# The heaviest expert's tokens 97 to 128: out of the overflow branch of their pair and into plain code

## The chip, the cores and the metric

The kernel runs on one core of a Trainium2 chip. The metric is the device time of one execution in microseconds (us), lower is better. The engines are named as in the profile: PE (TensorE matmul), PEld (its weight loads), DVE (VectorE), ACT (ScalarE), POOL (GpSimd), SP (SyncE, which here only issues DMAs).

## The reference, cut to what matters

Two layers; each is a mixer (convolutions in layer 0, gated MLP and attention in layer 1) and then a mixture of experts over 512 tokens of 1024 channels. Only the mixture is touched.

```
g_prob = softmax(xt @ rg_w + rg_b);  g_top, g_idx = top_k(g_prob, 1)     # 4 groups
e_top, e_idx = top_k(softmax(logits of the 8 experts of that group), 2)  # 2 experts a token
weights = g_top * e_top / sum(e_top)
...
hb = silu(xb @ w_gate[e]) * (xb @ w_up[e])     # 1024 -> 512
yb = hb @ w_down[e]                            # 512 -> 1024
y  = sum over the token's two experts of weight * yb
x  = LN(alpha * x + y)
```

All is float32. There are 32 experts; one has 3 matrices of 2 MB. How many tokens an expert gets is known only when the kernel runs.

## The kernel before, in words

A layer's 32 experts are taken in 16 pairs (`for g in range(NP)` in `experts`, L1056). A pair has a table of 128 slots. In twelve pairs each of the two experts has 64 slots. In the four pairs with column `COLS[g]` of at least `HEAVY` = 12, a heavily loaded expert (e = 0) has 96 slots and a lightly loaded one (e = 1) has 32. The experts are ordered by load at run time, so the heaviest of all (outside the first two pairs, which are fixed) is e = 0 of column 12, which is worked at g = 7.

In a pair PE runs, in this order: the gate projection (`proj2("g")`, 64 matmul instructions of 32 columns in a heavy pair), the up projection (`proj2("u")`), the adding of the previous pair's result into `acc` (`combine`: PE spreads rows by a one-hot matrix S, DVE adds), the transposes of the hidden rows in the middle of that (`hidden_T`), then the overflow branch `tc.If(v > 0)` (L1120), then the down projection (`down`) in two halves with the transposes of the next pair's tokens (`gather_T`) between them.

Tokens beyond the slots have a second table T2. `counts` (L621) writes into `nxi`, for each pair, 0 (nothing exceeds), 1 or 2 (one expert exceeds by up to 32) or 3 (more). If the value is over 0 the branch runs `overflow(v)`: it transposes the rows gathered into `xg2` (`gather2`, itself in a branch on POOL, one pair ahead), then either the full width (`wide`: `proj8`, `down8`) or one expert on 32 rows with the matrices cut into four strips that work side by side (`single(e)`: `proj1`, L840; `down1`, L881; `added1`, L872 and L875). The same code is emitted for g = 2 to 15 in both layers; a hint for PE's instruction fetch stands ahead of the up projection.

Weights come through a ring of nine 2 MB slots (`Stream`): matrix n of the sequence (six for a pair) takes the place of matrix n - 9. SP issues the loads in order, and a load waits until the last instruction that could read the old matrix has passed. The branch may read any of the pair's matrices, so a pair's two gate matrices and two up matrices are given back when PE has passed the branch, and the down matrices after the second half of `down`. What is given back at the branch of pair g are the places of the second up matrix and both down matrices of pair g + 1 and the first gate matrix of g + 2.

Of the kernel before, what the change touches and what calls it, by code (L numbers as in the profile page):

```python
# [7 lines left out]
F32 = mybir.dt.float32  # L8
# [35 lines left out]
def trunk(ctx: ExitStack, tc: tile.TileContext, a, out, layers=2, moe=True):  # L44
# [21 lines left out]
    def small(shape, name, dt=F32, **kw):  # L66
        return wk.tile([128] + list(shape), dt, name=name, **kw)
# [374 lines left out]
    class Router:  # L442
# [178 lines left out]
        def counts(self):  # L621
            c = self.rk[:, NT]
            big = wk.tile([128, NE, NE], F32, name="big", tag="xb")
            TT(big, self.at, bc(c[:, None, :], [NE, NE]), op=OP.mult)
            cs = small([NP, 2], "cs", tag="rcb")
            DVE.tensor_reduce(cs.rearrange("p g two -> p (g two)"), big, axis=AX.X, op=OP.add)
            over = small([2, NP, 2], "over", tag="scr")
            for i in range(2):
                TT(over[:, i], cs, lim[:, i], op=OP.is_gt)
            nxs = small([2 * NP + 1], "nxs")  # L630
            n, m = nxs[:, 0:NP], nxs[:, NP:2 * NP]
            mxc = small([NP], "mxc", tag="mxc")
            DVE.tensor_reduce(mxc, over[:, 1], axis=AX.X, op=OP.max)
            DVE.scalar_tensor_tensor(n, over[:, 0, :, 1], 2.0, over[:, 0, :, 0], op0=OP.mult, op1=OP.add)
            DVE.scalar_tensor_tensor(n, mxc, float(WIDE), n, op0=OP.mult, op1=OP.max)
            mxe = small([NP], "mxe", tag="mxc")
            DVE.tensor_reduce(mxe, c.rearrange("p (g two) -> p g two", two=2), axis=AX.X, op=OP.max)
            nx = small([NP, NTHR], "nx", tag="scr")
            TT(nx, bc(mxe[:, :, None], [NP, NTHR]), bc(thr[:, None, :], [NP, NTHR]), op=OP.is_gt)
            DVE.tensor_reduce(m, nx, axis=AX.X, op=OP.add)  # L640
            for g in FIRST:
                DVE.scalar_tensor_tensor(m[:, g:g + 1], mxe[:, g:g + 1], float(CAP), m[:, g:g + 1], op0=OP.is_gt, op1=OP.add)
            DVE.tensor_reduce(nxs[:, 2 * NP:], m, axis=AX.X, op=OP.max)
            nxi = small([2 * NP + 1], "nxi", I32)
            DVE.tensor_copy(nxi, nxs)
            return nxi
# [59 lines left out]
    def gather_T(src, gb, xt=None):  # L706
        xt = slots_T() if xt is None else xt
        transposed(src, lambda h, p: put_T(xt, gb, h, p))
        return xt
# [123 lines left out]
    def blocks4(p, f):  # L833
        for c in range(4):
            f(p[SUB * c:SUB * c + SUB], c)

    def proj1(tag, x, w, e):
        p = ptile(tag, (128, 128))
        for k in range(KD):
            blocks4(p, lambda o, c: PE.matmul(o, x[:, k, SUB * e:SUB * e + SUB], w[:, k, 128 * c:128 * c + 128],  # L840
                                              start=(k == 0), stop=(k == KD - 1)))
        return p
# [45 lines left out]
    def down8(hT, ww, wt, tk, own):  # L888
        S = onehot_S(tk)
        y = wk.tile([128, 2, 512], F32R, name="y2", tag="xb")  # L890
        ys = [(y[:, 0], y[:, 1]), tuple(wk.tile([128, 512], F32R, name="y3" + t, tag=t) for t in ("r", "q1"))]
        for h in range(2):
            scaled_parts(*ys[h], proj8("gu"[h], hT, ww, own, 4, slice(512 * h, 512 * h + 512)), wt)
        for h in range(2):
            for t in range(NT):
                added(t, h, S, ys[h])
# [76 lines left out]
    def when(nxi, i, above, engines=None):  # L973
        v = count(nxi, i, **({} if engines is None else {"engines": engines}))
        return v, tc.If(v > above)

    def experts(rt, ws, T1, pt, x1d, xt, xg, xg2, update, last, last2, lead, finish):
# [46 lines left out]
        def col(t, g):  # L1024
            return t[:, COLS[g]:COLS[g] + 1]

        def gather2(g):
            with when(nxi, COLS[g], 0, [ET.Pool])[1]:
                gather(xg2, x1d, col(T2.idx, g))

# [25 lines left out]
        for g in range(NP):  # L1056
            W = lambda j: ws.u[6 * g + j]
            own, own2 = EVEN if COLS[g] < HEAVY else ODD
            if g == NP - 1:
                crowded()  # L1060
                last()
            skip = f"skip{ws.l}_{g}"
            sg = gated(proj2("g", xt, W(0), W(1), own))
            if g == 0:
                onehot2()
            if g < 2:
                ws.load(6 * g + 2 + 9)
            tw = small([2], "tw")

            def either(v, wide, single):  # L1070
                with tc.If(v > WIDE - 1) as c:
                    wide()
                with c.Else():
                    with tc.If(v > 1) as c1:
                        single(1)
                    with c1.Else():
                        single(0)

            def overflow(v):
                h2 = wk.tile([128, 512], F32, name="h2", tag="r")  # L1080
                xo = gather_T(xg2, rt.gb, wk.tile([128, KD, 128], F32, name="xo", tag="xb"))
                hT2 = wk.tile([128, 4, 128], F32, name="hT2", tag="q0")

                def wide():
                    ACT.activation(h2, proj8("g", xo, (W(0), W(1)), own2), AF.Silu)
                    DVE.tensor_mul(h2, h2, proj8("u", xo, (W(2), W(3)), own2))
                    hidden2_T(h2, hT2, 4)

                def single(e):
                    b = (0, 1) if own2 == EVEN[1] else (2, 1)  # L1090
                    s = slice(0, 128)
                    ACT.activation(h2[:, s], proj1("g", xo, W(e), b[e]), AF.Silu)
                    DVE.tensor_mul(h2[:, s], h2[:, s], proj1("u", xo, W(2 + e), b[e]))
                    hidden2_T(h2, hT2, 1)
                    r = slice(SUB * b[e], SUB * b[e] + SUB)
                    for i, src in enumerate((T2.tk, T2.wt)):
                        blocks4(tw, lambda o, c: DVE.tensor_copy(o[:, i:i + 1], col(src, g)[r]))
                either(v, wide, single)
                either(v, lambda: down8(hT2, (W(4), W(5)), col(T2.wt, g), col(T2.tk, g), own2),
                       lambda e: down1(hT2, W(4 + e), tw[:, 1:2], tw[:, 0:1]))  # L1100
            if g:
                S = onehot_S(col(T1.tk, g - 1))
                if g == NP - 1:
                    combine(S, *prev, (0, 1))
            if g > 1:
                v = count(nxi, COLS[g])
                tc.mark_branch_hint_location(skip, v > 0, engines=[ET.PE])
            pu = proj2("u", xt, W(2), W(3), own)
            h = hidden(sg, pu)
            if g == 0:  # L1110
                first_weights()
            else:
                combine(S, *prev, range(2 if g == NP - 1 else 0, CM if g < NP - 1 else NT))
            hT = hidden_T(h)
            if g == 0:
                ws.ids = rt.order()
            if 0 < g < NP - 1:
                combine(S, *prev, range(CM, NT))
            if g > 1:
                with tc.If(v > 0, label=skip, preferred_fallthrough_block=True):  # L1120
                    overflow(v)
            ws.load(6 * g + 4 + 9)
            if g == NP - 1:
                last2()
            if 0 < g < NP - 1:
                gather2(g + 1)
            if g == NP - 2:
                most = count(nxi, 2 * NP)
                tc.mark_branch_hint_location(f"most{ws.l}", most > 0, engines=[ET.PE])
            if g == NP - 1:  # L1130
                S = onehot_S(col(T1.tk, g))
            if g < NP - 1:
                wt = wt0 if g == 0 else col(T1.wt, g)
                y = down(hT, W(4), W(5), wt, halves=(0,), own=own)
                xt = gather_T(xg, rt.gb)
                if g == 0:
                    nxi, rest = picks()
                if g + 2 < NP:
                    gather(xg, x1d, col(T1.idx, g + 2))
                prev = down(hT, W(4), W(5), wt, y, (1,), own)  # L1140
                if g == 0:
                    rest()
            else:
                end, y = Last(lead), None
                for h in range(2):
                    y = down(hT, W(4), W(5), col(T1.wt, g), y, (h,), own)
                    end.half(h, S, *y)
            ws.load(6 * g + 6 + 9)
# [525 lines left out]
```

## Time and profile before

| | us |
|---|---|
| three runs | 1456.77, 1446.28, 1455.97 (median 1455.97) |
| profiled execution: its own time | 1450.72 |
| profiled execution: its span | 1448.9 |

The profiled execution lies between the lowest and the highest of the three runs. Times below are us from the start of its span. Layer 0's experts fill about 203 to 690 us, layer 1's about 947 to 1420. A row of the timeline gives start, length, engine, line, operation, tiles written and read, the count of merged instructions, and in brackets how long the engine was idle before it and what ended that.

### The profile page before, as it was taken

How to read it: one execution, taken by the hardware profiler on the slowest of the kernel's cores; microseconds unless marked ns; L12 is line 12 of the kernel's file. 1: busy time of each engine (PE TensorE's matmuls, PEld its weight loads, DVE VectorE, ACT ScalarE, POOL GpSimd, SP SyncE). 2: the span in 40 equal slices, each digit the busy share in tenths (PEclk: the TensorE clock that was granted, in tenths of full speed). 3: DMA queues.
4: the chain of work that ended last, by engine and by line, in shares of the span. 5: the costliest groups of instructions: out<-in, count | busy, mean ns of one | idle time of the engine just before them, and what ended most of it. 6: DMA issues, size and time to landing. Idle time of an engine off the chain costs nothing. (4 is left out here: it accounts for less than half of the span.)

```text
span 1448.9 us, 19205 instructions
## 1 busy us (share of the span) xinstructions
PE 1326.9 (92%) x7119; PEld 698.7 (48%) x7121; DVE 675.9 (47%) x1387; ACT 368.3 (25%) x694; POOL 294.0 (20%) x261
## 2 busy tenths in 40 slices
PE   9989999998978999988899999999998999988984
PEld 6767764343333433333576767744433343333331
DVE  7998588232222332232718555784322232322336
ACT  5545631111101111111524455521111111111101
POOL 5785610000000000000463229300000000000002
PEclk9999999999998999999999999999999999999997
DMA  7505479999997899999700018789999999999971
GB/s 293 232 5 241 166 262 425 420 424 422 420 400 301 355 426 423 422 420 378 283 1 1 23 66 325 268 320 423 421 423 424 423 423 422 425 421 422 420 304 59
DMA packets 56693, 461.19 MB, mean 318 GB/s; under 512 B 8661, under 2 KB 9301, under 8 KB 33089
## 3 DMA queue, kind: packets, MB, share of 16 engines
q1 hardware_dynamic: 51184, 449.96, 75.4%
q0 software_dynamic: 4464, 7.79, 1.5%
q8 instruction: 101, 1.65, 0.5%
q10 hardware_dynamic: 864, 1.13, 0.2%
q14 instruction: 80, 0.65, 0.1%
HBM read 461.04 MB, written 6.29 MB: 323 GB/s over the span
## 5 line engine op out<-in xcount | busy, mean ns | idle before, releaser
L745 PE MATMUL pu<-w,xt 128*64 128x512 f32 (+1 forms) x1280 | 247.8, 606 | 31.8 <-DMA w<-in_w_up_dram 31.8
L745 PE MATMUL py<-w,hT 128*64 128x512 f32 (+1 forms) x1280 | 242.3, 611 | 18.4 <-issue 7.3
L745 PE MATMUL pg<-w,xt 128*64 128x512 f32 (+1 forms) x1280 | 235.1, 600 | 10.9 <-ACTq L1033 10.9
L760 DVE TENSOR_TENSOR h<-sg,pu 128x512 f32<-128x512 f32 x32 | 22.0, 688 | 379.9 <-issue 342.7
L690 POOL DMA_INDIRECT xg<-x1d,idx x29 | 28.7, 990 | 794.3 <-PE m L439 711.6
L745 PEld LDWEIGHTS pu<-w,xt 128*64 128x64 f32 (+1 forms) x1280 | 75.4, 129 | 194.1 <-issue 149.0
L798 DVE TENSOR_TENSOR acc<-acc,m 128x512 f32<-128x512 f32 x240 | 148.6, 680 | 17.9 <-PE m L790 15.7
L745 PEld LDWEIGHTS pg<-w,xt 128*64 128x64 f32 (+1 forms) x1280 | 77.5, 127 | 163.4 <-issue 144.6
L745 PEld LDWEIGHTS py<-w,hT 128*64 128x64 f32 (+1 forms) x1280 | 71.7, 128 | 150.7 <-issue 146.8
L779 DVE SCALAR_TENSOR_TENSOR y<-py,wt,y 128x512 fp32r<-128x512 f32 x64 | 48.0, 750 | 194.6 <-ACT y L778 194.6
L778 ACT ACTIVATE y<-py,wt 128x512 fp32r<-128x512 f32 x64 | 44.0, 687 | 295.1 <-PE py L745 295.1
L789 PE MATMUL m<-y,S 128*128 128x512 f32 x248 | 106.2, 428 | 0.0
L109 POOL TENSOR_TENSOR wl<-win,wh 128x512 fp32r<-128x512 f32 x64 | 84.5, 1335 | 67.7 <-ACT wh L108 67.5
L790 PE MATMUL m<-y,S 128*128 128x512 f32 x248 | 97.8, 394 | 0.0
L768 ACT ACTIVATE hT<-m 128x512 f32<-128x512 f32 x32 | 19.1, 598 | 304.9 <-PE m L766 282.9
L109 POOL TENSOR_TENSOR wl<-wo,wh 128x512 fp32r<-128x512 f32 x64 | 82.3, 1314 | 34.8 <-ACT wh L108 34.4
L755 ACT ACTIVATE sg<-pg 128x512 f32<-128x512 f32 x32 | 19.1, 597 | 219.0 <-PE pg L745 219.0
L789 PEld LDWEIGHTS m<-y,S 128*128 128x128 f32 x248 | 46.6, 188 | 39.7 <-issue 26.9
L128 PE MATMUL m<-xh,wl 128*128 128x512 f32 x144 | 58.7, 408 | 3.1 <-POOL wl L109 3.1
L127 PE MATMUL m<-xh,wh 128*128 128x512 f32 x144 | 58.3, 405 | 0.8 <-ACT wh L108 0.8
L129 PE MATMUL m<-xl,wh 128*128 128x512 f32 x144 | 57.9, 402 | 0.0
L108 ACT ACTIVATE wh<-win 128x512 fp32r<-128x512 f32 x64 | 38.9, 625 | 49.0 <-PE pg L129 13.4
(445 smaller groups left out, 1858.8 us busy)
## 6 DMA issues: line engine op xcount, KB each, us to landing
w<-in_w_gate_dram SPq DMA_DIRECT2D x64, 2048.0 KB, 25.0
w<-in_w_up_dram SPq DMA_DIRECT2D x50, 2048.0 KB, 18.3
w<-in_w_down_dram SPq DMA_DIRECT2D x50, 2048.0 KB, 21.2
w<-in_w_up_dram SPq DMA_DIRECT2D x40, 512.0 KB, 24.7
w<-in_w_down_dram SPq DMA_DIRECT2D x40, 512.0 KB, 22.3
win<-in_w_in_dram SPq DMA_DIRECT2D x18, 512.0 KB, 7.6
wo<-in_w_out_dram SPq DMA_DIRECT2D x4, 2048.0 KB, 12.2
w<-in_w_up_dram SPq DMA_DIRECT2D x8, 1024.0 KB, 16.2
```

Of the source, the lines that this page charges most:

```text
L108: ACT.activation(h, src, AF.Copy)
L109: POOL.tensor_tensor(l, src, h, op=OP.subtract)
L127: PE.matmul(p, wh[:, j], xh[:, k], start=(k == 0), stop=False)
L128: PE.matmul(p, wl[:, j], xh[:, k], start=False, stop=False)
L129: PE.matmul(p, wh[:, j], xl[:, k], start=False, stop=(k == KD - 1))
L690: POOL.indirect_dma_start(out=dst, out_offset=None, in_=x1d, in_offset=bass.IndirectOffsetOnAxis(ap=idx_col, axis=0), bounds_check=T - 1, ...
L745: PE.matmul(p[w * c:w * c + w], x[:, w * c:w * c + w], ww[own[w * c // SUB]], **kw)
L778: ACT.activation(yh[:, s], p, AF.Copy, scale=wt)
L779: DVE.scalar_tensor_tensor(yl[:, s], p, wt, yh[:, s], op0=OP.mult, op1=OP.subtract)
L789: PE.matmul(p, S[:, t * 128:(t + 1) * 128], yh[:, s], start=start, stop=False)
L790: PE.matmul(p, S[:, t * 128:(t + 1) * 128], yl[:, s], start=False, stop=True)
L798: DVE.tensor_add(acc[:, t, s], acc[:, t, s], p)
```

## The change

For column 12 (`top`), e = 0 of T2 is always computed in plain code, spread over iteration g = 7: the gather is no longer in a branch; the copies of token numbers and weights (`single_in`), the transposes of the gathered rows and `proj1` for the gate come between the gate and the up projection; `proj1` for the up matrix, the product and one transpose come between `hidden_T` and the rest of `combine`; `down1` comes after `combine`, ahead of the branch. The branch stays, with the full width only, for the case that e = 1 exceeds its 32 slots; it then leaves out the block that the plain code has done. `counts` gets one more small instruction, which sets the value of column 12 to 3 if e = 1 exceeds and else to 0.

```
+            TS(n[:, HEAVY:HEAVY + 1], over[:, 0, HEAVY:HEAVY + 1, 1], float(WIDE), None, op0=OP.mult)
...
         def gather2(g):
+            if COLS[g] == HEAVY:
+                gather(xg2, x1d, col(T2.idx, g))
+                return
...
+            top = COLS[g] == HEAVY
+            def single_in(e):
+                b = ((0, 1) if own2 == EVEN[1] else (2, 1))[e]
+                for i, src in enumerate((T2.tk, T2.wt)):
+                    blocks4(tw, lambda o, c: DVE.tensor_copy(o[:, i:i + 1], col(src, g)[SUB * b:SUB * b + SUB]))
+                return b
...
             def either(v, wide, single):
+                if top:
+                    wide()
+                    return
...
+            if top:
+                b = single_in(0)
+                xo = gather_T(xg2, rt.gb, wk.tile([128, KD, 128], F32, name="xo", tag="xb"))
+                h2 = wk.tile([128, 128], F32, name="h2", tag="r")
+                ACT.activation(h2, proj1("g", xo, W(0), b), AF.Silu)
             if g > 1:
                 v = count(nxi, COLS[g])
                 tc.mark_branch_hint_location(skip, v > 0, engines=[ET.PE])
...
             hT = hidden_T(h)
+            if top:
+                DVE.tensor_mul(h2, h2, proj1("u", xo, W(2), b))
+                p2 = ptile("g", (128, 128))
+                PE.transpose(p2, h2, ident)
+                hT2 = wk.tile([128, 1, 128], F32, name="hT2", tag="q0")
+                ACT.activation(hT2[:, 0], p2, AF.Copy)
...
             if 0 < g < NP - 1:
                 combine(S, *prev, range(CM, NT))
+            if top:
+                down1(hT2, W(4), tw[:, 1:2], tw[:, 0:1])
             if g > 1:
                 with tc.If(v > 0, label=skip, preferred_fallthrough_block=True):
                     overflow(v)
```

## Rows read from the trace of the kernel before

**Rows 1.** The page: GB/s in 40 equal slices of the span (36.2 us each).

```profile
GB/s 293 232 5 241 166 262 425 420 424 422 420 400 301 355 426 423 422 420 378 283 1 1 23 66 325 268 320 423 421 423 424 423 423 422 425 421 422 420 304 59
```

**Rows 2.** SP's waits in layer 0's experts (us in total, times, longest).

```profile
SPq L964 <- PEq L1120: 141.6, 11, 19.3
```

**Rows 3.** Windows: length, busy time of engines, PEclk, DMA share, GB/s.

```profile
422.00:434.00 12.00, 6.74 (x129) 5.49 (x129) 1.48 (x10) 0.55 (x2) 0.00 (x0) 0.72 0.88 350
...
450.00:461.00 11.00, 11.00 (x78) 3.61 (x72) 3.17 (x7) 2.77 (x6) 0.99 (x1) 0.97 0.40 129
467.00:479.00 12.00, 11.85 (x57) 5.78 (x54) 5.56 (x9) 0.77 (x2) 0.00 (x0) 1.00 0.37 130
...
202.64:653.66 451.02, 417.54 (x2413) 172.16 (x2411) 164.02 (x326) 60.55 (x122) 17.04 (x17) 0.97 0.96 399
946.51:1381.18 434.67, 405.79 (x2215) 164.63 (x2216) 156.11 (x307) 58.85 (x118) 16.00 (x16) 0.99 0.99 414
```

**Rows 4.** Timeline of SP: weight loads; a long merged row ends with the second load.

```profile
398.79 29.94 SPq L964 DMA_DIRECT2D w<-in_w_up_dram  x2
...
433.40 23.70 SPq L964 DMA_DIRECT2D w<-in_w_gate_dram  x2
457.61 17.84 SPq L964 DMA_DIRECT2D w<-in_w_up_dram  x2
...
1145.12 18.45 SPq L964 DMA_DIRECT2D w<-in_w_up_dram  x2
```

**Rows 5.** Timeline of the branch at g = 7 in layer 0.

```profile
418.01 1.05 PE L439 MATMUL m<-ident,xg 128*128 128x128 f32 x8
...
419.46 1.36 DVE L704 TENSOR_SCALAR xo<-m,gb 128x128 f32<-128x128 f32 x4
...
424.67 3.64 PE L840 MATMUL pg<-w,xo 128*32 128x128 f32 x64 [5.60 <-issue]
...
430.72 1.50 PE L840 MATMUL pu<-w,xo 128*32 128x128 f32 x44 [1.15 <-issue]
...
432.34 0.29 DVE L1093 TENSOR_TENSOR h<-h,pu 128x128 f32<-128x128 f32 x1 [11.53 <-PE pu L840]
...
437.10 3.60 PE L881 MATMUL m<-w,hT 128*32 128x256 f32 x32 [4.08 <-issue]
...
444.55 1.82 PE L872 MATMUL m<-y,S 32*128 32x256 f32 x8 [1.37 <-DVE acc L875]
446.29 5.83 PE L745 MATMUL py<-w,hT 128*32 128x512 f32 x32
```

**Rows 6.** Timeline of PE and PEld: pair g = 7, up projection to branch, both layers.

```profile
404.63 1.03 PE L745 MATMUL pu<-w,xt 128*32 128x512 f32 x4
...
406.74 7.06 PE L745 MATMUL pu<-w,xt 128*32 128x512 f32 x60 [1.08 <-DMA w<-in_w_up_dram]
...
413.73 0.50 PE L789 MATMUL m<-y,S 128*128 128x512 f32 x1
...
1151.66 0.16 PEld L745 LDWEIGHTS pu<-w,xt 128*32 128x32 f32 x8 [0.92 <-DMA w<-in_w_up_dram]
...
1158.65 0.50 PE L789 MATMUL m<-y,S 128*128 128x512 f32 x1
...
1163.25 3.64 PE L745 MATMUL py<-w,hT 128*32 128x512 f32 x32
```

**Rows 7.** Windows in the branch, for PEclk (the third figure from the end).

```profile
424.60:428.30 3.70, 3.63 (x70) 3.36 (x73) 0.00 (x0) 0.00 (x0) 0.00 (x0) 0.50 0.79 332
430.70:432.30 1.60, 1.50 (x44) 1.23 (x43) 0.00 (x0) 0.00 (x0) 0.00 (x0) 1.00 0.99 410
```

**Rows 8.** The gather for g = 7 in layer 0, and its time from issue to landing.

```profile
390.23 0.99 POOL L690 DMA_INDIRECT xg<-x1d,idx  x1 [22.43 <-DVE acc L798]
...
xg<-x1d,idx POOLq DMA_INDIRECT x1, 7.3
```

**Rows 9.** Timeline of PE: after a branch that was not taken, g = 4, layer 0.

```profile
328.28 2.78 PE L745 MATMUL py<-w,hT 128*32 128x512 f32 x10 [3.38 <-PEq L1120]
```

More of the change, by code (lines that the diff above doesn't have):

```diff
@@ L1082, in overflow @@
                 hT2 = wk.tile([128, 4, 128], F32, name="hT2", tag="q0")
+                tk2, wt2 = col(T2.tk, g), col(T2.wt, g)
+                if top:
+                    rest2 = small([2], "rest2", tag="mxc")
+                    DVE.memset(rest2, 0.0)
+                    for b in (0, 1, 3):
+                        r = slice(SUB * b, SUB * b + SUB)
+                        DVE.tensor_copy(rest2[r, 0:1], tk2[r])
+                        DVE.tensor_copy(rest2[r, 1:2], wt2[r])
+                    tk2, wt2 = rest2[:, 0:1], rest2[:, 1:2]
                 def wide():
@@ L1089, in single @@
                 def single(e):
-                    b = (0, 1) if own2 == EVEN[1] else (2, 1)
+                    b = single_in(e)
                     s = slice(0, 128)
-                    ACT.activation(h2[:, s], proj1("g", xo, W(e), b[e]), AF.Silu)
-                    DVE.tensor_mul(h2[:, s], h2[:, s], proj1("u", xo, W(2 + e), b[e]))
+                    ACT.activation(h2[:, s], proj1("g", xo, W(e), b), AF.Silu)
+                    DVE.tensor_mul(h2[:, s], h2[:, s], proj1("u", xo, W(2 + e), b))
                     hidden2_T(h2, hT2, 1)
-                    r = slice(SUB * b[e], SUB * b[e] + SUB)
-                    for i, src in enumerate((T2.tk, T2.wt)):
-                        blocks4(tw, lambda o, c: DVE.tensor_copy(o[:, i:i + 1], col(src, g)[r]))
                 either(v, wide, single)
-                either(v, lambda: down8(hT2, (W(4), W(5)), col(T2.wt, g), col(T2.tk, g), own2),
+                either(v, lambda: down8(hT2, (W(4), W(5)), wt2, tk2, own2),
                        lambda e: down1(hT2, W(4 + e), tw[:, 1:2], tw[:, 0:1]))
@@ L1118, in experts @@
                 combine(S, *prev, range(CM, NT))
+            if top:
+                down1(hT2, W(4), tw[:, 1:2], tw[:, 0:1])
             if g > 1:
```

## The prediction, made before the changed kernel was run

> **What bounds the kernel now.** First the row of GB/s: in both expert stages the core moves 420 to 426 GB/s in almost every slice [rows 1]. One matrix of 2.097 MB then takes 4.95 us, a pair of six 29.7 us, and whatever PE does within that costs nothing. The exception is three slices of layer 0 (400, 301, 355), some 400 to 507 us. Second, SP's waits: inside the experts it waits longest for PE's branch [rows 2], so weights are late only when PE is late at that branch. Third, that stretch in windows. At 424 GB/s the three holes lost 12 x 74 / 424 = 2.1 us, 11 x 295 / 424 = 7.7 us and 12 x 294 / 424 = 8.3 us [rows 3], 18.1 us together. As a check: from the first gate matmul to the last group of weight loads layer 0 took 451.02 us and layer 1 434.67 [rows 3], 16.4 us less for the same work. So the loss goes through to the end, and 16.4 to 18.1 us is all that can be won.
>
> Fourth, SP's timeline ties each hole to a release. The second up load of pair 8 went out only at 428.73 (398.79 + 29.94), just as the first gate projection of the branch had ended; the load after the first gate matrix of pair 9 at 457.1; the second up load of pair 9 at 475.45 [rows 4]. The branch was taken only in layer 0, in the arm for e = 0 alone: `single`'s 128-column form of L840 stands there once, and layer 1 goes on to `down` 4.6 us after its up projection, as any skipped pair [rows 5, 6]. So the change replaces a taken branch in layer 0 and adds computation in layer 1, where none ran.
>
> **What it removes.** In layer 0 PE left `combine` at 418 us and reached `down` at 446.29. Of these 28 us, 5.60, 1.15 and 4.08 are idle time put down to "issue" [rows 5], with no data outstanding: PE had no instructions. Plain code should have none of that: 10.8 us.
>
> [...]
>
> **What it adds ahead of the release.** The gate and up matrices of pair 7 still go back only when PE has passed the branch, since the branch can still read them; and all new PE work stands ahead of it. I count PE's delay to that point.
>
> A1, before the up projection: the eight transposes and the ACT and DVE copies took 420.82 - 418.01 = 2.8 us from first to last, and PE has nothing else to do meanwhile; then 64 instructions of `proj1`, which took 1.50 / 44 = 34 ns each at full clock and 3.64 / 64 = 57 ns at half clock [rows 5, 7]. At full clock 2.2 us, sum 5.0 us. Part of it fills a wait: PE idled for the up matrix 1.7 us in layer 0 (406.74 - 404.63 less four instructions of 0.11) and 0.9 us in layer 1 [rows 6]. Net 3.3 and 4.1 us. The lower bound is 1 us less, if `proj1` starts on the first copied slices.
>
> A2, after `hidden_T`: 64 x 34 ns = 2.2 us, the wait for DVE's product (0.29 us and a hand-over [rows 5]) and one transpose: 3.0 us.
>
> A3, `down1`'s 32 matmuls: they took 3.60 us in the branch, like the first `proj1` after an idle time. Their strips have 256 columns, and the 512-column ones of the pair's up projection take (413.73 - 406.74) / 60 = 0.117 us [rows 5, 6], so half of that at full clock, 1.9 us.
>
> A4, from the end of `down1` (440.70) to `down` (446.29): 5.6 us [rows 5]. It holds ACT's and DVE's scaling and eight additions on DVE, whose pace made PE wait 1.37 us for a bank. None of it is branching but the last jump; I take 5.2 us, between 4.6 (full clock, no jump) and 5.6.
>
> Sum 13.4 us in layer 0, 14.2 in layer 1. Without overflow work the second up load of pair 8 would go out 4.60 + 0.32 us after 413.73, at 418.65 [rows 4, 6]; now it goes out at 432.05. That is 3.3 us later than the 428.73 which cost 2.1 us: a hole of 5.4 us. In layer 1 the up matrix landed at 1151.66; the point like 428.73 is 22.0 us later (428.73 - 406.74), 1173.65. The release moves from 1163.57 to 1177.8, 4.1 us past that point: a hole of 6.2 us where there was none.
>
> A second hole shouldn't follow. At the release four loads go out and two more after `down`, 29.7 us of traffic, and PE needs less for a pair: even with a slow start it came from 446.29 to the release of 475.45 in 29.2 us [rows 4, 5]. The margin is thin, and a rival rests on it.
>
> **What is priced at nothing.** The gather on POOL is issued a pair ahead and landed 7.3 us after 390.23 in layer 0, at 397.5, while the transposes now want it at about 404.6 [rows 6, 8]: 7 us of cover; if that goes, PE waits ahead of A1, and the release with it. In layer 1 it is new: 1 us of POOL, which waits 22 us idle, and at most 0.5 MB (1.2 us of traffic at 424 GB/s; most slots there are empty and move nothing, so I take 0). The small DVE instruction in `counts`: at most a few tenths, once a layer, while PE is busy and DMA full. The eight tiny copies on DVE sit behind the gate projection, when DVE is idle. The branch's skip stays as it was.
>
> **Sum.** 18.1 removed, 5.4 and 6.2 added: 6.5 us gained; 4.8 by the check of 16.4. I take 6. Against the profiled execution's own 1450.72 us (span 1448.9, 1.8 around it) that is 1444.7. The four times at hand, 1446.3 to 1456.8, have their middle at 1453.3, which gives 1447; I forecast 1446. A measurement of this kernel can tell about 1% (14.5 us) from no change.
>
> **Rivals.**
>
> (a) The new work overlaps better: `proj1` runs slice by slice behind the copies and the additions drain while `combine` still runs, so that PE is 3 us earlier per layer. The holes fall to 2.4 and 3.2 us, the gain rises to 12.5: about 1438 on the profiled execution. For it: DVE and ACT have room there. Against: the last additions need `down1`'s result, and only their banks set PE's pace.
>
> (b) The new work runs slower than I take it: PEclk is 0.50 as in the branch [rows 7]. A1, A2 and A3 then cost 1.5, 1.5 and 1.7 us more, the holes grow by 4.7 each, and the gain is -2.9: 1453.6. Or PE's skip is not fetched in time, as once in layer 0 (3.38 us [rows 9]); the hint now stands some 250 PE instructions further ahead of it. In one layer the gain is 3.1, in both -0.3. Against half clock: in the trace it came after PE had been idle for 5.6 us, and here it is never idle for 3.
>
> [...]
>
> (c) Slower: the clock falls in A1 to A4 as in (b) and stays down through `down` of pair 7, so that PE misses the thin margin and a second hole opens in each layer. `down`'s first half took 5.83 us there against 3.64 [rows 5, 6]; both halves slow cost 4.4 us, less 0.5 of margin: about 4 us a layer on top of (b), 1461. It decides if the release comes later than about 436 us in layer 0.
>
> (d) The change doesn't do what it says: the branch is taken as well, since e = 1 exceeds 32. The arm taken in the trace was that for e = 0 alone, so the value now is 0. Some 25 us on top, 1470.
>
> **How the numbers follow.** The forecast (a gain of 3 to 10 us) has 0.58, (a) 0.17, (b) 0.18, (c) 0.05, (d) 0.02. From (a), 1438 or a little under, to (b) with the higher of the base times, the range is 1436 to 1457. Faster by over 1% needs a gain of 14.5 us, nearly all there is: the far part of (a), and the spread of the base times, 0.16. Slower by over 1%: (c), (d) and the spread, 0.08. Within 1%: 0.76.
>
> **What would show it.** Right: no idle "issue" of some us at g = 7 in layer 0; holes in GB/s after the branch of g = 7 in both layers, about 5 us each, and none a pair later; SP's second up load of pair 8 about 13 us after the point of a skipped pair; layer 0's experts 13 us shorter and layer 1's 6 us longer. Wrong: no hole in layer 1 (then A1 to A4 are hidden, and the gain nears 17); a hole of 9 us or more (clock or fetch); or a release that no longer waits for the branch.

## The result, and the profile after

| | before | after |
|---|---|---|
| median of 8 runs each, us | 1456.28 | 1442.19 |
| lowest to highest, us | 1446.28 to 1457.60 | 1439.13 to 1445.43 |
| profiled execution: its own time (span), us | 1450.72 (1448.9) | 1442.83 (1440.9) |

The ratio is 0.9929, with a 95% interval of 0.9909 to 0.9948: 10 us (8 to 13) faster. That is a gain, but under the 1% that the prediction set as its bound for faster. The medians lie 14.1 us apart, because five of the eight runs of before stand at 1456 to 1458 us and three at 1446 to 1451; the text goes by the ratio on record and its interval. The two profiled executions differ by 7.9 us.

The page's row of GB/s has lost the dip of layer 0 [rows 1]:

```profile
GB/s 294 234 5 212 175 243 428 419 424 422 419 403 412 422 419 426 422 418 354 206 1 1 23 133 315 257 338 421 420 425 424 421 394 420 427 422 422 423 301 59
```

What is left of it is a shallow place (403, 412), and layer 1 has a new one (394). In windows of 10 us, around g = 7 in each layer, and over each layer's experts from the first gate matmul of the first pair to that of the last:

```profile
204.06:655.10 451.04, 420.16 (x2446) 174.97 (x2445) 167.61 (x337) 64.14 (x131) 16.98 (x17) 0.98 0.99 411
...
420.00:430.00 10.00, 7.36 (x74) 5.14 (x74) 7.54 (x14) 0.75 (x2) 0.00 (x0) 0.96 0.95 401
430.00:440.00 10.00, 9.85 (x67) 3.71 (x69) 4.14 (x9) 2.08 (x5) 0.99 (x1) 0.69 0.87 344
440.00:450.00 10.00, 10.00 (x60) 3.14 (x54) 1.21 (x3) 1.28 (x2) 0.00 (x0) 1.00 1.01 400
...
936.20:1384.82 448.62, 421.48 (x2447) 173.47 (x2446) 167.53 (x337) 64.09 (x131) 17.10 (x17) 0.98 0.99 412
...
1160.00:1170.00 10.00, 8.43 (x56) 3.80 (x60) 5.27 (x10) 1.70 (x5) 0.47 (x1) 0.83 0.84 323
1170.00:1180.00 10.00, 10.00 (x62) 3.15 (x56) 2.19 (x6) 1.11 (x4) 0.52 (x1) 1.00 1.00 413
```

Below, the "hole" of a layer is the sum of (424 - GB/s) x length / 424 over the windows below full rate. Here it is (23 + 80 + 24) x 10 / 424 = 3.0 us in layer 0, where before lost 18.1 [rows 3], and (101 + 11) x 10 / 424 = 2.6 us in layer 1, where before lost nothing. Measured between the same two gate matmuls, layer 0 took 463.7 us before (201.73 to 665.46) and 451.1 now, layer 1 446.6 (946.51 to 1393.08) and 448.6. So layer 0 gave 12.6 us and layer 1 took back 2.1. The first expert matmul also started 2.3 us later (204.06 against 201.73, behind work that the change doesn't touch); 12.6 - 2.1 - 2.3 = 8.2 us, where the two spans differ by 8.0, and the stretches between the layers and behind them agree within 0.3 us.

PE's timeline at g = 7 in layer 0, where [rows 5] showed the branch:

```profile
405.82 1.09 PE L439 MATMUL m<-ident,xg 128*128 128x128 f32 x8
407.07 2.35 PE L841 MATMUL pg<-w,xo 128*32 128x128 f32 x64 [0.16 <-ACT xo L703]
409.23 7.32 PE L746 MATMUL pu<-w,xt 128*32 128x512 f32 x64
...
418.05 1.95 PE L841 MATMUL pu<-w,xo 128*32 128x128 f32 x64
420.49 0.33 PE L1146 MATMUL pg<-ident,h 128*128 128x128 f32 x1 [0.48 <-DVE h L1144]
...
423.55 1.93 PE L882 MATMUL m<-w,hT 128*32 128x256 f32 x32
426.13 0.90 PE L873 MATMUL pg<-y,S 32*128 32x256 f32 x2 [0.65 <-ACTq L1156]
...
429.24 1.81 PE L873 MATMUL m<-y,S 32*128 32x256 f32 x8 [1.37 <-DVE acc L876]
```

No idle time of PE is put down to "issue" here. `down` follows at 431.20, and the release shows on SP's own timeline (the merged row ends with the second up load of pair 8, as in [rows 4]):

```profile
402.15 29.36 SPq L965 DMA_DIRECT2D w<-in_w_up_dram  x2
...
1134.31 28.91 SPq L965 DMA_DIRECT2D w<-in_w_up_dram  x2
```

402.15 + 29.36 = 431.51 in layer 0, 1163.22 in layer 1. And something is there that before didn't have: two issue waits of PE in the last pairs of layer 0, g = 13 and 14. An issue wait, below, is idle time of PE that the profile puts down to "issue" or to PEq, PE's sequencer.

```profile
611.77 2.31 PE L746 MATMUL py<-w,hT 128*32 128x512 f32 x17 [3.23 <-issue]
...
642.37 2.73 PE L746 MATMUL py<-w,hT 128*64 128x512 f32 x10 [2.72 <-issue]
```

### The profile page after: what moved, and what is told of

Read it like the earlier page. It is cut to its first block, busy times and chain, and to the rows that moved or that the text cites. A ratio compares the mean times of both kernels' runs of the same rounds, so it can differ in the third digit from the quotient of the medians.

```text
span 1440.9 us, 19633 instructions
## 1 busy us (share of the span) xinstructions
PE 1333.4 (93%) x7322; PEld 705.9 (49%) x7322; DVE 684.5 (48%) x1412; ACT 370.3 (26%) x701; POOL 294.7 (20%) x262
## 3 DMA queue, kind: packets, MB, share of 16 engines
q0 software_dynamic: 4608, 7.79, 1.5%
## 5 line engine op out<-in xcount | busy, mean ns | idle before, releaser
L746 PE MATMUL pu<-w,xt 128*64 128x512 f32 (+1 forms) x1280 | 244.2, 607 | 19.8 <-DMA w<-in_w_up_dram 19.8
L746 PEld LDWEIGHTS pu<-w,xt 128*64 128x64 f32 (+1 forms) x1280 | 78.3, 129 | 176.3 <-issue 143.2
L799 DVE TENSOR_TENSOR acc<-acc,m 128x512 f32<-128x512 f32 x240 | 148.6, 680 | 19.3 <-PE m L791 17.3
L790 PEld LDWEIGHTS m<-y,S 128*128 128x128 f32 x248 | 46.8, 189 | 39.3 <-issue 26.9
L791 PEld LDWEIGHTS m<-y,S 128*128 128x128 f32 x248 | 46.9, 189 | 7.9 <-DVE y L780 1.0
```

Of the source, the lines that this page charges most:

```text
L746: PE.matmul(p[w * c:w * c + w], x[:, w * c:w * c + w], ww[own[w * c // SUB]], **kw)
L790: PE.matmul(p, S[:, t * 128:(t + 1) * 128], yh[:, s], start=start, stop=False)
L791: PE.matmul(p, S[:, t * 128:(t + 1) * 128], yl[:, s], start=False, stop=True)
L799: DVE.tensor_add(acc[:, t, s], acc[:, t, s], p)
```

## The experiments

Theory 1 is the prediction's: the loss is the hole that PE's lateness at the release of g = 7 makes in the weight traffic; only what stands ahead of the release counts. Its rivals: (2) only the waits in the taken branch counted (5.60, 1.15 and 4.08 us), and the computation is hidden anyway; (3) what counts is PE's whole lag against the loads already issued, wherever in the pair it arises. A last theory (L) came up on the way: some issue waits depend on where the code lies, not on what it does. Ratios are against the kernel before on the same chip, with the 95% interval; 0.1% is 1.45 us.

**No overflow work at all.** The kernel before, with the counts' new line alone; the heaviest expert's tokens 97 to 128 are left out.

```
+            TS(n[:, HEAVY:HEAVY + 1], over[:, 0, HEAVY:HEAVY + 1, 1], float(WIDE), None, op0=OP.mult)
```

> The kernel before, with the count of column 12 set so that its branch is never taken: it leaves out the heaviest expert's tokens 97 to 128 in layer 0, so it bounds what can be won. Theory 1 (the whole loss is the holes in the weight traffic, 18 us before and 5 to 6 in the changed kernel): 16 to 18 us under the kernel before, ratio 0.988, 5 us under the changed kernel, no hole in either layer. Theory 2 (the gain is the fetch stalls of the taken branch, 10.8 us, and the computation itself is hidden): about the changed kernel's time, ratio 0.9925.

Measured: 1438.99 us, ratio 0.9888 (0.9867 to 0.9910). Windows at g = 7 in layer 0:

```profile
420.00:430.00 10.00, 9.91 (x80) 3.55 (x82) 4.22 (x10) 2.77 (x6) 0.99 (x1) 1.00 1.00 424
430.00:440.00 10.00, 7.64 (x32) 2.39 (x30) 0.26 (x1) 0.60 (x1) 0.00 (x0) 0.93 1.00 420
```

No hole. Layer 0 took 446.7 us, layer 1 446.3: 17.0 us less than before in layer 0. That is all there is to be won, and after stands 4.4 and 2.3 us above it. Theory 2 would have put this kernel level with after. Against theory 2 this run alone says little: its interval touches that of after (up to 0.9910, from 0.9909), and below, with the code moved, after comes down to 446.8 us in layer 0 as well. The run with the plain code in one piece decides.

**The change in layer 0 alone.** Layer 1 keeps the branch, which is never taken there. The new lines in `counts` and `gather2` get the same condition.

```
-            top = COLS[g] == HEAVY
+            top = COLS[g] == HEAVY and not ws.l
```

> The change in layer 0 alone; layer 1 keeps the branch, which isn't taken there. Theory 1: the hole of about 2.7 us in layer 1 goes, the rest stays: 2 to 3 us under the changed kernel, ratio 0.991. Theory 2 (new work in layer 1 is hidden): the changed kernel's time, ratio 0.993.

Measured: 1444.03 us, ratio 0.9936 (0.9914 to 0.9957); no better than after. Layer 1's hole was gone (419 and 426 GB/s there), but its stage took 448.1 us against 448.6; it had an issue wait of 3.14 us near the layer's end (at 1343.99) that after didn't have. So this run doesn't price the hole of layer 1, and no theory so far foresaw it. Layer 0 took 454.6 us, 3.5 more than in after, although its hole was the same 2.9 us (352, 392 and 406 GB/s); it too has waits at g = 13 and 14, of 3.25 and 2.37 us. That is where theory L began.

**All of the plain code in one piece ahead of the branch.** The same work at the place where the branch had it, without the jump: nothing overlaps the pair's own projections.

```
             if 0 < g < NP - 1:
                 combine(S, *prev, range(CM, NT))
+            if top:
+                b = single_in(0)
+                ...
+                ACT.activation(h2, proj1("g", xo, W(0), b), AF.Silu)
             if top:
                 DVE.tensor_mul(h2, h2, proj1("u", xo, W(2), b))
```

> All of the new plain code in one piece ahead of the branch, behind combine, not spread over the iteration. Theory 1: PE now stands idle for the copies, no longer fills its wait for the up matrix, and reaches the branch some 3 us later in each layer; the holes grow by as much: 5 to 6 us over the changed kernel, ratio 0.997. Theory 2 (only the fetch stalls mattered): the changed kernel's time, ratio 0.993.

Measured: 1448.63 us, ratio 0.9972 (0.9954 to 0.9991). The interval lies apart from that of after (up to 0.9948), where theory 2 expected the same time. The profiled execution was the fastest of twelve (1443.06 us), so the stages and holes of this kernel are those of its best case. Windows, layer 0:

```profile
420.00:430.00 10.00, 7.74 (x177) 4.96 (x169) 3.88 (x15) 1.41 (x5) 0.00 (x0) 1.00 0.77 324
430.00:440.00 10.00, 8.47 (x57) 3.79 (x60) 5.34 (x10) 1.64 (x5) 0.40 (x1) 0.83 0.64 234
```

The hole is 6.8 us in layer 0 and 7.6 in layer 1. Against before this is the cleanest look at the jump: same work, same place, and the hole went from 18.1 to 6.8, by 11.3 us where the three waits in the branch had been 10.8. PE reached `down` 35.7 us after the pair's first gate matmul, 12.9 us sooner than in before (48.6); what goes beyond the 10.8 is mostly faster matmuls, as those of `down1` (1.93 us here, 3.60 in the branch). The hole also stands elsewhere. In before the taken branch gave its matrices back from inside, one after the other, so before lost only 2.1 us at this release and 16.0 behind it [rows 3, 4]; here the release came when PE had passed the branch, at 433.28, and the whole hole stands there. Against after this kernel shows what the spreading is worth: some 6 us by the ratios, but only 2.2 us by the stages of the profiled executions (451.2 and 450.7 us against 451.1 and 448.6).

**`down1` behind the branch.** 7.7 us of PE's time (423.55 to 431.20 in after) move past the release. The edit also gives `hT2` another buffer.

```
-            if top:
-                down1(hT2, W(4), tw[:, 1:2], tw[:, 0:1])
             if g > 1:
                 with tc.If(v > 0, label=skip, preferred_fallthrough_block=True):
                     overflow(v)
+            if top:
+                down1(hT2, W(4), tw[:, 1:2], tw[:, 0:1])
```

> down1 of the new code moved behind the branch, so that the gate and up matrices go back 7.6 us earlier; the work is the same. Theory 1 in its narrow form (only the release of this pair counts): both holes go, 5 to 6 us under the changed kernel, ratio 0.989. Theory 3 (what counts is how far PE is behind in all; the stock of issued loads lasts a fixed time): the hole at pair 7 goes and one of 2 us or so opens at the release of pair 8 instead; 0 to 2 us under the changed kernel, ratio 0.992.

Measured: 1443.41 us, ratio 0.9937 (0.9912 to 0.9961): no gain. The release came at 422.74 and the hole there closed; one of 3.7 us opened a pair later:

```profile
420.00:430.00 10.00, 6.31 (x70) 4.38 (x68) 7.07 (x13) 0.47 (x1) 0.00 (x0) 0.95 0.99 410
430.00:440.00 10.00, 10.00 (x65) 3.05 (x68) 3.35 (x8) 2.08 (x5) 0.99 (x1) 0.71 1.00 420
...
450.00:460.00 10.00, 9.85 (x46) 4.87 (x44) 4.77 (x8) 0.60 (x1) 0.00 (x0) 1.00 0.75 319
460.00:470.00 10.00, 10.00 (x52) 3.96 (x50) 3.96 (x9) 2.77 (x6) 0.99 (x1) 1.00 0.95 374
```

PE was as late as in after, only at the next release. Layer 1 shows the same: a hole of 2.5 us a pair later (316 GB/s from 1190 to 1200 us), and 448.7 us as in after (448.6). This speaks for theory 3 against the "ahead of the release" of theory 1. The total alone would not decide it: layer 0 took 454.8 us with issue waits of 3.09 and 2.32 us at g = 13, of the kind that after has too.

**`down1` split.** Its matmuls and scaling behind the branch, the first four additions behind the first half of `down`, the last four behind the second half, so that PE needn't stand idle for DVE's additions (1.37 us in after).

```
+            if top:
+                S, y2 = down1a(hT2, W(4), tw[:, 1:2], tw[:, 0:1])
...
                 y = down(hT, W(4), W(5), wt, halves=(0,), own=own)
+                if top:
+                    for n in range(4):
+                        added1(2 * (n // 4), n % 4, "gummmmmm"[n], S, y2)
...
```

> The changed kernel with down1 taken apart: its matmuls and scaling stand behind the branch, four of the eight additions behind the first half of down, four behind the second, so that PE has other work while ACT scales and DVE adds. Same computation. Theory 3 (what counts is how far PE is behind in all): PE loses its idle time in the additions, about 3.5 us a layer, the holes of 3.0 and 2.7 us close; 3 to 6 us under the changed kernel, ratio 0.990. Rival (the gaps in the additions are DVE's and only move to the next pair's transposes and scaling): the time of the changed kernel, 0.993, with PE waiting for banks in the second half of down.

Measured: 1441.94 us, ratio 0.9942 (0.9926 to 0.9957). No window at g = 7 or 8 is below 413 GB/s, so the hole is gone in both layers; layer 1 took 446.5 us, as with no overflow work. But layer 0 took 453.7. PE's timeline has the reason at g = 13:

```profile
607.93 2.31 PE L746 MATMUL py<-w,hT 128*32 128x512 f32 x17 [3.00 <-PEq L1164]
612.64 3.05 PE L746 MATMUL py<-w,hT 128*32 128x512 f32 x15 [2.41 <-issue]
```

These are 5.4 us of waits in a pair that the edit doesn't touch. The weight rate was 359 GB/s from 640 to 650 us, but it falls there in other kernels too: from 630 to 670 us it was 428, 409, 373 and 333 in after, and 403, 390, 273 and 372 in the faster split kernel with 64 (below).

**Doubling the lag, ahead of the branch and behind it.** After, with 46 idle bf16 matmuls at g = 7 in both layers, once just ahead of the branch and once just behind it.

```
             if top:
                 down1(hT2, W(4), tw[:, 1:2], tw[:, 0:1])
+                keep_warm(46)          # first kernel
             if g > 1:
                 with tc.If(v > 0, label=skip, preferred_fallthrough_block=True):
                     overflow(v)
+            if top:
+                keep_warm(46)          # second kernel
```

> The changed kernel with 46 idle matmuls (bf16, result unread, 9.8 us of PE at full clock) just ahead of the branch of column 12, in both layers. Theories 1 and 3: each microsecond beyond the stock of issued loads costs one; the hole at pair 7 grows by 9.8 us in each layer, 19 to 20 us over the changed kernel, ratio 1.006. Rival (PE has 3 us to spare in each of the eight pairs that follow and catches up): no more than a few us, 0.994.

> The same 46 idle matmuls just behind the branch, in both layers, so that pair 7's gate and up matrices go back as early as in the changed kernel. Theory 3: the hole at pair 7 stays at 3 us and a second one of about 9 us opens at the release of pair 8; 18 us over the changed kernel, ratio 1.0055, nearly as ahead of the branch. Theory 1 in its narrow form (only what stands ahead of the release counts): the changed kernel's time, 0.993.

Measured: ahead 1464.78 us, ratio 1.0088 (1.0066 to 1.0109); behind 1461.03, ratio 1.0062 (1.0042 to 1.0083). The idle matmuls took longer than the 9.8 us that the expectations gave them, 11.90 us ahead of the branch and 12.19 behind it in layer 0:

```profile
428.14 11.90 PE L148 MATMUL m<-onesb 128*128 128x512 bf16 x46
```

Windows of the first (the hole of 14.7 us, 11.7 more than in after):

```profile
420.00:430.00 10.00, 7.83 (x77) 4.72 (x76) 8.39 (x15) 0.47 (x1) 0.00 (x0) 0.95 0.72 301
430.00:440.00 10.00, 10.00 (x41) 4.06 (x39) 0.00 (x0) 0.00 (x0) 0.00 (x0) 0.88 0.01 2
440.00:450.00 10.00, 9.85 (x81) 3.55 (x82) 2.82 (x7) 2.77 (x6) 0.99 (x1) 1.00 0.89 344
```

and of the second, where the hole at the release of g = 7 stays at 2.4 us and the rest, 9.5 us, opens a pair later (380, 176 and 315 GB/s from 450 to 480 us):

```profile
420.00:430.00 10.00, 7.62 (x75) 5.39 (x76) 7.67 (x14) 0.75 (x2) 0.00 (x0) 0.96 0.95 403
430.00:440.00 10.00, 8.77 (x32) 3.74 (x32) 1.92 (x4) 0.00 (x0) 0.00 (x0) 0.70 0.90 357
...
460.00:470.00 10.00, 10.00 (x48) 4.91 (x45) 3.55 (x6) 0.70 (x2) 0.00 (x0) 1.00 0.42 176
```

Against after the two are 1.6% and 1.3% slower, 12 and 10 us for each layer, and their intervals overlap. Theory 3 holds in the main: a lag of 12 us more on PE is lost in full ahead of the release, and some four fifths of it behind, most of it at the next release. The narrow form of theory 1, the time of after, is out by 19 us. In layer 1 of the second kernel 5.2 us were lost at this release and 11.0 behind it; PE had waited 5.10 and 2.93 us behind skipped branches at g = 4 and 5.

**Moving the code.** 64 idle matmuls of two columns at the start of the program. With one weight load each (the page of after counts 7322 matmuls and 7322 weight loads) they move all of PE's later code by 128 instructions. The experts start no later for it (201.2 to 202.0 us; 201.7 in before).

```
     keep_warm(W0)
+    pad = ptile("m")
+    for _ in range(64):
+        PE.matmul(pad[:, 0:2], onesb[:, 0:1].to_broadcast([128, 128]), onesb[:, 0:2], start=True, stop=True)
```

In after:

> The changed kernel with 64 tiny matmuls (two columns, result unread) at the very start of PE's program, which move every later PE instruction by 128 places; at the start PE waits for the first loads, so they should cost nothing by themselves. Theory L (where the fetch stalls of PE fall is a matter of where the branches lie in the fetched blocks; in the changed kernel they fall on pairs 13 and 14 of layer 0, where the stock is short, and cost 4 to 5 us): the waits at pairs 13 and 14 (3.2 and 2.7 us) go or move to another pair, and layer 0's experts change by 3 to 6 us, one way or the other; with them gone 1438, ratio 0.990. Rival (the waits belong to those pairs whatever the layout): the same waits at the same pairs, time as the changed kernel, 0.993.

In the split kernel, with 64 and with 32:

> The version with down1 taken apart, moved by the same 128 places. It had no hole at pair 7 or 8 but waits of 3.0 and 2.4 us at pair 13 of layer 0. Theory L: these move; if to a pair in the middle of the layer, layer 0's experts take 447 to 449 us instead of 453.7 and the ratio falls to about 0.990. Rival: the same waits, 0.994.

> As the run before, moved by 64 places. Theory L: another set of waits again; a time between 0.989 and 0.995 that follows from where they fall. Rival: the same waits, 0.994.

In the kernel before:

> The kernel before with 64 idle two-column matmuls at the start of the program, which move all of PE's code by 128 instructions. If the 10.8 us of fetch waits in the branch of pair 7 come from the jumps themselves, they stay near 11 us, the holes stay near 18 us, layer 0 stays near 463 us, and the time stays within 0.4% of the kernel before (the skip waits at pair 4, 3.4 and 1.3 us, may go: they stand at a place that costs little). Rival: those waits too hang on where the code lies. Then they change by several us, the holes with them, and the ratio leaves 0.996 to 1.004; part of the change's gain would then be a matter of layout.

| kernel | us | ratio | layer 0, us | layer 1, us |
|---|---|---|---|---|
| after | 1442.19 | 0.9929 (0.9909 to 0.9948) | 451.1 | 448.6 |
| after, 64 | 1437.81 | 0.9912 (0.9885 to 0.9939) | 446.8 | 449.5 |
| split | 1441.94 | 0.9942 (0.9926 to 0.9957) | 453.7 | 446.5 |
| split, 64 | 1434.55 | 0.9892 (0.9865 to 0.9918) | 446.8 | 446.1 |
| split, 32 | 1438.19 | 0.9907 (0.9879 to 0.9935) | 446.5 | 450.1 |
| before, 64 | 1459.13 | 1.0042 (1.0022 to 1.0062) | 470.7 | 446.5 |

In after and in the split kernel, with 64, the waits of g = 13 and 14 in layer 0 are gone, and layer 0 is down to the 446.7 us of the kernel without overflow work. For the split kernel the two intervals lie apart; for after they overlap, and the evidence is the stage's time in one execution each. With 32 the waits stand elsewhere. Two fell into g = 7 of layer 1 (the second of 4.25 us) and opened a hole of 5.1 us a pair later, where the split kernel had none. In layer 0 one stands at g = 3, one at g = 8 and two at g = 12, and layer 0 takes 446.5 us all the same:

```profile
302.14 5.62 PE L749 MATMUL py<-w,hT 128*64 128x512 f32 x16 [5.23 <-PEq L1167]
...
574.29 3.65 PE L749 MATMUL py<-w,hT 128*64 128x512 f32 x16 [2.93 <-PEq L1167]
579.94 1.09 PE L442 MATMUL m<-ident,xg 128*128 128x128 f32 x8 [1.99 <-issue]
```

The profile gives these waits no cause beyond "issue" and "PEq". That PE lacked instructions there, or was fetching them, is the author's reading; what is shown is that the profile has nothing that PE waited for, and that the waits move with the code. Each kernel has one trace, so that they recur in every execution isn't shown directly. But after, the change in layer 0 alone, in one piece, `down1` behind and split all have one at g = 4 and one at g = 13 of layer 0, and the moved versions of after and split have neither. Every edit here moves the code behind it, so a difference of some 4 us a layer between two of these kernels can't be credited to the edit alone.

In the kernel before, the shift made the taken branch dearer. Its timeline, where [rows 5] had 5.60, 1.15 and 4.08:

```profile
425.93 1.50 PE L843 MATMUL pg<-w,xo 128*32 128x128 f32 x20 [5.62 <-issue]
431.98 2.56 PE L843 MATMUL pg<-w,xo 128*32 128x128 f32 x42 [4.56 <-issue]
...
444.56 3.22 PE L884 MATMUL m<-w,hT 128*32 128x256 f32 x32 [6.12 <-issue]
```

The waits are 16.3 us instead of 10.8, the hole, in windows of 10 us from 420 to 490, grew to 25.6 us (18.1 in before, 18.4 in the same windows), and layer 0 by 7.0 us. A wait of 3.21 us at g = 13 is also new. The expectation's first case fails here, and its rival holds: how long PE waited in the taken branch depended on where the code lay, too. The change stays a gain at both places of the code: after against before is 0.993 as they stand, and 0.9912 / 1.0042 = 0.987 with both moved (two chips). The split kernel with 64 is the best of all, with no hole at g = 7:

```profile
420.00:430.00 10.00, 8.46 (x97) 4.51 (x99) 4.67 (x9) 1.86 (x4) 0.02 (x1) 1.00 1.01 428
430.00:440.00 10.00, 10.00 (x78) 3.44 (x72) 6.71 (x14) 1.50 (x4) 0.97 (x1) 1.00 0.99 410
```

By the ratios it is as fast as the kernel that leaves the tokens out (0.9892 and 0.9888). Against after with the same shift, on the same chip, it is 3.3 us lower, with intervals that overlap.

**Holes against stage times.** Laid side by side, the kernels show what a hole costs. Late waits are issue waits at g = 13 or 14. 446.5 us is the middle of the eight stages that have neither a hole of more than 1.5 us nor late waits (446.1 to 446.8; in layer 0 no overflow work and the split kernel with 64 and with 32, in layer 1 no overflow work, the split kernel, the same with 64, before and before with 64). The table has all the others.

| kernel, layer | hole, us | stage, us | over 446.5 |
|---|---|---|---|
| before, layer 0 | 18.1 | 463.7 | 17.2 |
| 46 matmuls ahead, layer 1 | 17.0 | 462.2 | 15.7 |
| 46 matmuls behind, layer 1 | 16.2 | 461.9 | 15.4 |
| 46 matmuls ahead, layer 0 | 14.7 | 460.0 | 13.5 |
| 46 matmuls behind, layer 0 | 11.9 | 456.3 | 9.8 |
| in one piece, layer 1 | 7.6 | 450.7 | 4.2 |
| after with 64, layer 1 | 6.3 | 449.5 | 3.0 |
| split with 32, layer 1 | 5.1 | 450.1 | 3.6 |
| after with 64, layer 0 | 3.5 | 446.8 | 0.3 |
| after, layer 1 | 2.6 | 448.6 | 2.1 |
| `down1` behind, layer 1 | 2.5 | 448.7 | 2.2 |
| *with one late wait of about 3 us:* | | | |
| before with 64, layer 0 | 25.6 | 470.7 | 24.2 |
| in one piece, layer 0 | 6.8 | 451.2 | 4.7 |
| change in layer 0 alone, layer 1 | 0 | 448.1 | 1.6 |
| *with late waits of 5.4 to 6.0 us:* | | | |
| `down1` behind, layer 0 | 3.7 | 454.8 | 8.3 |
| after, layer 0 | 3.0 | 451.1 | 4.6 |
| change in layer 0 alone, layer 0 | 2.9 | 454.6 | 8.1 |
| split, layer 0 | 0 | 453.7 | 7.2 |

Without late waits a hole costs its length less 0.3 to 3.4 us. The last loads of layer 0 ran below full rate: from 650 to 670 us 373 and 333 GB/s in after, 354 and 384 in after with 64, 273 and 372 in split with 64, 271 and 409 in split with 32, and 389 and 322 from 660 to 680 us in before. That a stage gives something back there is argued from this and not shown. With late waits of 5.4 to 6.0 us the stage is longer by 1.6 to 7.2 us more than its hole. Waits as long at g = 12 cost nothing: 2.93 and 1.99 us in split with 32, layer 0 (446.5 us), and 5.20 us in before with 64, layer 1 (446.5). PE's next pair shows the difference. In the split kernel with 64 and no late waits PE waits for the up matrix of g = 14; in split, behind its late waits, it doesn't:

```profile
622.35 7.08 PE L749 MATMUL pu<-w,xt 128*64 128x512 f32 x30 [2.70 <-DMA w<-in_w_up_dram]
```

```profile
627.64 7.04 PE L746 MATMUL pu<-w,xt 128*64 128x512 f32 x32
```

So from g = 14 on only some 2.7 us of waiting for weights were left to take up a delay, and what exceeds them reaches the end of the stage. That accounts for a part of the 7.2 us, not for all.

## Why the prediction was right, and where it wasn't

The forecast of 1446 us against 1442.19 was right in place and mechanism. As a difference it was 6 us, and 10 were measured by the ratio; that layer 0 came out almost as forecast is luck, as the sum below shows.

**What it removes.** Right. The waits of the taken branch (10.8 us) are the larger part of the hole of 18.1: without the jump and with the same work in the same place, 11.3 us of the hole went; with the waits 5.5 us longer, it grew by 7.5 and layer 0 by 7.0. That plain code has none of these waits was the author's estimate. In the plain code at g = 7 of after it held: no idle time ahead of `down` is put down to "issue" in either layer. As a rule it isn't shown: the waits of 3.23 and 2.72 us at g = 13 and 14 stand inside `down`, in straight code, each behind 1.9 us of matmuls that follow a skipped branch.

**A1 to A4.** Right within 1 us each. A1 took 4.1 us, since `proj1` started on the first copied slices after 0.16 us (its lower bound was 4.0, the value taken 5.0); A2 2.5 (3.0), from 418.05 to 420.57, where `combine` goes on; A3 1.9 (1.9); A4 from 425.48 to 431.20, 5.7 (5.2). The release came at 431.51 (432.05) in layer 0, 33.3 us after the pair's first gate matmul, and 33.1 us after it in layer 1 (34.1).

**The added holes: the term that was mis-sized.** 5.4 and 6.2 us were predicted, 3.0 and 2.6 measured. PE's release, 1 us earlier after the gate matmul, explains 1 us of that. The rest is PE's place against the loads, which the prediction took over from the kernel before: there the up matrix of pair 7 landed 9.0 and 7.9 us after the pair's first gate matmul. What holds still is the time from a landing to the moment when the issued loads run out (the release less the hole), as worked out from PE's waits. It is 19.3 to 20.2 us from the up matrix of pair 7 (before and before with 64 in layer 0, in one piece in both layers) and 50.2 to 50.7 us from that of pair 6 (after in layer 1, after with 64 in both, before with 64 in layer 0). Counted so, PE's gate matmul in layer 1 of after stood 2.6 us further ahead of the loads than the prediction had it, and they ran out that much later after it. In layer 0 they ran out 1.4 us later after it; there PE waits for no up matrix in pairs 4 to 7, so that the cause is the same isn't shown. After with 64, layer 1, shows the other side. These are the two waits for the up matrix of pair 6, in after and in after with 64:

```profile
1110.33 7.08 PE L746 MATMUL pu<-w,xt 128*64 128x512 f32 x30 [0.95 <-DMA w<-in_w_up_dram]
```

```profile
1102.99 9.85 PE L749 MATMUL pu<-w,xt 128*64 128x512 f32 x30 [3.81 <-DMA w<-in_w_up_dram]
```

In after the gate matmul of pair 7 follows 19.8 us after that landing, in after with 64 only 25.0 us after it: PE was behind by 5.2 us more. With the code moved the release came 31.9 us after the gate matmul, sooner than in after (33.1), and still the hole was 6.3 us instead of 2.6. The prediction also charged each hole in full: in layer 1 2.6 us of hole went with 2.1 of stage, and in after with 64 the 3.5 us of layer 0 with 0.3.

**The sum.** Layer 0 was to be 12.7 us shorter, and is 12.6; but its smaller hole would have made that 15, and the late waits took the difference back. Layer 1 was to be 6.2 longer, and is 2.1. The 10.5 us that remain agree with the gain by the ratio; the profiled pair shows 8, because of the 2.3 us ahead of the experts.

**Counting PE's delay only to the release.** As a rule this is wrong, though all of the change's work stood ahead of the release and so no number of the sum rested on it. `down1` behind the branch and 46 matmuls behind the branch moved the hole a pair on and left most of it. What counts is PE's whole lag against the loads that are out. A second hole, which rival (c) put down to a slow `down`, came in these two kernels from that lag.

**The rivals.** (a) gave 1438, and the gain went part of the way there, but not by overlap: PE's terms were within 1 us. (b) and (c): the granted clock dipped (0.96 and 0.69 in the two windows from 420 us), but the matmuls of A1 to A3 ran about as priced (2.35, 1.95 and 1.93 us; priced 2.2, 2.2 and 1.9). `down`'s first half, behind them, was slow (6.05 us, and 5.83 in the branch's wake before), and even so no second hole came. The wait behind the skipped branch at g = 4 is still there (2.67 us, to [rows 9]) and costs nothing that can be seen: the kernel without overflow work has it too (3.39 us), and its layer 0 takes the same 446.7 us as the shifted kernels, which don't. (d): the branch was not taken.

**What was priced at nothing.** Right, as far as the traces show. PE's transposes at g = 7 follow the gate projection with no wait for the gather, in both layers, and the queue q0 (software_dynamic on the page) has 144 packets more in after, with 30 gathers instead of 29: 4608 instead of 4464, and it moved 7.79 MB in both kernels.

**What it didn't foresee.** The waits of 3.23 and 2.72 us at g = 13 and 14, worth some 4 us of layer 0 by the shifted kernel (451.1 to 446.8). The chances had no case for code that moves.

**Open.** Why the waits fall where they do: the trace shows no addresses of the code. How often they recur from execution to execution. Why late waits of nearly the same length cost 1.6 us beyond the hole in after and 4.6 to 7.2 in three other kernels. And why the stretch between the layers, which no edit touches, took 281 us in most of the profiled executions and 285 to 286 in three (no overflow work and both with 46 matmuls).

## What to carry to other kernels

Where a ring of loads runs at full rate (some 424 GB/s here), count the lag of the engine that frees its places against the loads already out: below that stock a delay was free here, above it cost its length less 0.3 to 3.4 us, and moving work past one release only moved the hole to the next. Start the count at a landing that the engine waits for, not at a matmul of its own. Work that is nearly always needed may be cheaper in plain code than in a taken branch (ratio 0.9972 here), and cheaper still cut into pieces that fill the waits of the work around it (0.9929); where it isn't needed, as in layer 1 here, it costs something (2.1 us). Before crediting a gain of half a per cent to an edit, shift the code and measure again, because the position alone was worth about as much here (0.42% and 0.5%).

## What the runs showed of the hardware that was not expected

- Moving PE's code by 128 instructions, with 64 idle matmuls at the start and nothing else, made one kernel 0.42% (0.22 to 0.62) slower and took another from 0.9942 to 0.9892. The waits of a taken branch went from 5.60, 1.15 and 4.08 us to 5.62, 4.56 and 6.12.
- Behind a branch that is not taken PE waited up to 5.25 us (46 matmuls ahead, 1074.55 us) and up to 4.25 us more in an issue wait 5.7 us on (split with 32, 1151.46 and 1157.19 us). A delay of 5 us at g = 12 cost the stage nothing, at g = 13 up to 7 us. At the 28 branches of after, none of them taken, PE has four waits that end with the branch, of 2.67, 0.79, 0.21 and 0.86 us.
